# A mixture of experts behind a Hyena and Fourier mixer: the two last experts from different groups, multiplied in undivided float32, with the final norm's reads and writes moved

## The chip, the cores and the metric

The kernel runs on one core of a Trainium2 chip. The metric is the device time of one execution in microseconds, as a median of several runs, smaller being better. A profiled execution gives the trace that the rows below come from; its span is counted from its first instruction. The engines are TensorE (PE in the rows, PEld for its weight loads), VectorE (DVE), ScalarE (ACT), GpSimd (POOL) and SyncE (SP). SP and GpSimd also issue transfers, and each takes its instructions in its own order.

## What is computed

One block on 2048 rows of 1024 float32 numbers: a mixer (long convolution by FFT on half of the channels, a Fourier transform on the other half) added to the input, then a mixture of experts, then a norm over each row.

```python
g_sel = jnp.argmax(g_logits, axis=-1)              # one of 4 groups per row
top_l, top_i = lax.top_k(e_logits, TOP_K)          # 2 of its 8 experts
weight = p_group[:, None] * jax.nn.softmax(top_l, axis=-1)
...
    a = xb @ w_gate[e]                             # 1024 x 512
    u = xb @ w_up[e]
    y = (jax.nn.silu(a) * u) @ w_down[e]           # 512 x 1024
...
x = x + hierarchical_moe(rmsnorm(x, norm2_g[i]), w_group[i], ...)
return rmsnorm(x, final_g)
```

A row belongs to one group, and both of its experts are of that group. So two experts of different groups have no row in common.

## The kernel before, in words

The mixer takes the first 960 us or so and leaves the normed rows in DRAM (XR) and the sum to which the experts' results are added (X2). Then the 32 experts follow one another. Their order is found on the chip (`order`, line 1164): experts are ranked by their number of rows, and slots 0 to 31 of the kernel take them in an order that mixes those with many rows (ranks 2 to 17) with the others (`_ranks`, line 60). Below, "expert 28" means slot 28. Slots 0 and 1 are experts 0 and 1; slots 30 and 31 have the two smallest ranks' places. A slot covers 128 rows; one of the first 18 ranks has an overflow tile of 32 more (`over`, `turn_o`, `turn_so`, the second half of `extra`), whose result is added by a scatter of its own (line 1607). Rows beyond that are left to a loop at the end (line 1726), which runs as often as blocks are left over, here not at all.

For a slot e the work is this. `gather` fetches its rows from XR; `turn` (line 1531) transposes them on TensorE and splits them into a rounded part xh (a copy on ScalarE) and a rest xl (a subtraction on VectorE), both float32r, the format that TensorE multiplies in one pass. `gate_up` (line 1556) takes 8 weight tiles of 128 x 1024, each holding two slices of the contraction, and multiplies each slice three times: xh h, xh l, xl h. `cut` (line 1393) makes h and l of a weight tile: h by a copy on ScalarE (line 1397), l by a subtraction on VectorE or, for some tiles and for every second one of the last 24, on GpSimd (line 1398). The gate goes through Silu and is multiplied by the up part (lines 1573, 1574); `turn_s` transposes and splits the result; `down` (line 1642) takes 4 tiles, again with three products each. The result is scaled by the rows' weights (line 1660) and added to X2 by a scatter that accumulates (line 1661, issued by GpSimd).

`take` hands out weight tiles in the order of `seq`, which is that of `turns`: (e, 0) is gate and up of e, (e, 1) its down. Up to slot 29 the down part of e - 1 stands behind gate and up of e, with the transposes of later slots in its middle (`between`). At each call `take` also starts loads up to 28 tiles ahead and cuts 2 tiles ahead, and calls the next closure of `ends`, if there is one. A float32 tile lies in one of 16 buffers "wr" or 8 others, and the loads are issued on SP.

The end. Slots 30 and 31 don't add to X2 by an accumulating scatter. `ahead` gathers their rows of X2 (za), `finish` (line 1481) adds the weighted result to it, writes za back to X2, and norms it to oa. For the other rows `bulk` (line 1435) makes 30 steps: all 2048 rows are read from X2 in 16 blocks (`read`, into buffers "wr", line 1443), squared with their sum on ScalarE (line 1433), and in groups of four the roots are made (`rsq`, line 236) and the rows scaled on VectorE (line 1459) and written to the output by SP (line 1460). Steps start behind expert 29's down part, one at each `take`, and those left over follow at the end. Last, two scatters put oa of slots 30 and 31 over their rows of the output (line 1717); each waits for all that was written there before.

Instructions reach an engine mostly in the order in which the code makes them; the framework that allocates buffers and sets the semaphores may put a ready one ahead of one that its plan sees waiting. The line `tc.add_manual_dep(... "cuts first")` holds a square back behind cuts.

Of the kernel before, what the change touches and what calls it, by code (L numbers as in the profile page):

```python
# [46 lines left out]
FIRST = 14  # L47
NLAST = 2
# [4 lines left out]
TAIL_CUTS = tuple(range(360, 384, 2))  # L53
# [6 lines left out]
def _ranks():  # L60

    n, few = NE - NFIX - NLAST, NE - NOV - NLAST
# [142 lines left out]
def build(tc, I, out, dbg=None, upto=99):  # L205
# [4 lines left out]
    with es:  # L210
# [641 lines left out]
        turns += [(z - 1, 1), (z, 0), (z, 1), (z + 1, 0), (z + 1, 1)]  # L852
# [53 lines left out]
        with ExitStack() as e3:  # L906
# [202 lines left out]
            with tc.tile_pool(name="pd", bufs=1, side="right", reuse_waits="tile") as pd_:  # L1109
# [54 lines left out]
                def order():  # L1164
# [8 lines left out]
                    V.scalar_tensor_tensor(so[:, 0], cnt, float(NE), srt[:, 0:NE], op0=ALU.mult, op1=ALU.add)  # L1173
                    V.tensor_tensor(so[:, 1], so[:, 0], srt[:, 2 * NE:3 * NE], op=ALU.mult)
# [214 lines left out]
        if True:  # L1389
# [3 lines left out]
            def cut(n):  # L1393
# [4 lines left out]
                x = (G if n in POOL_CUTS + TAIL_CUTS else V).tensor_tensor(l, raws[n], h, op=ALU.subtract)  # L1398
# [4 lines left out]
            done, cuts = [NRAW, 0, 0], []  # L1403

            def take():
# [14 lines left out]
                return hl.pop(n), raws.pop(n)  # L1420
# [14 lines left out]
            def bulk():  # L1435
# [3 lines left out]
                scales = []  # L1439
# [5 lines left out]
                def sq(o):  # L1445
# [3 lines left out]
                    x = square(xts[o], fss[g][0][:, o - g:o - g + 1])  # L1449

                    tc.add_manual_dep(x.ins, cuts[-1].ins.name, ORDER_ONLY, reason="cuts first")
                    if o == g + n - 1:
                        rsq(fss[g][1], fss[g][0], 1.0 / D, mp, n, "q%d" % n)
                        scales.extend(range(g, g + n))

                def scale(o):
# [24 lines left out]
            def finish(e, py, za):  # L1481

                ss = mp.tile([P, 1], F32, name="zs")
                ra = mp.tile([P, 1], F32, name="zra")
# [136 lines left out]
            def turn_s(e):  # L1621
# [5 lines left out]
                for j in range(4):  # L1627
                    T.transpose(pt[:, j, :], s[:, P * j:P * j + P], ident)  # L1628
# [209 lines left out]
```

## Time and profile before

| | us |
|---|---|
| median of 3 runs (1729.77 to 1732.64) | 1729.94 |
| profiled execution, timed | 1725.99 |
| its span | 1724.2 |
| TensorE busy | 1601.3 (93%) |
| VectorE busy | 1224.2 (71%) |
| ScalarE busy | 1039.7 (60%) |
| GpSimd busy | 476.6 (28%) |
| granted clock, mean share of 2.4 GHz | 0.961 |

Busy times are those of instructions; two that overlap on an engine count once. The span ends when the last engine has passed the closing barrier. A row of the timeline has the start, the duration of what was merged into it, engine, line, operation, result <- operands, the count, and in brackets the idle time before it with what ended that. X stands for X2 in the rows, out_y for the output.

### The profile page before, as it was taken

The numbers are of one execution on the slowest core, as the hardware profiler recorded it, in microseconds if no ns is written. First come the engines' busy times: TensorE is split into PE (matmuls) and PEld (weight loads), VectorE is DVE, ScalarE is ACT, GpSimd is POOL, SyncE is SP. The second block draws the span as 40 slices with busy tenths as digits, with TensorE's granted clock in tenths as the row PEclk, the third lists the DMA queues.
The fourth block names the chain that finished last, engine by engine and source line by source line (L and its number), as shares of the span: only waits on it lengthen the run. The fifth ranks groups of instructions, "written<-read, shape, count | busy, mean of one in ns | idle before, by whom it ended". The sixth has DMA issues, their size and how long they took to land.

```text
span 1724.2 us, 27277 instructions
## 1 busy us (share of the span) xinstructions
PE 1601.3 (93%) x9043; PEld 1233.2 (72%) x9043; DVE 1224.2 (71%) x2105; ACT 1039.7 (60%) x1694; POOL 476.6 (28%) x513
## 2 busy tenths in 40 slices
PE   7999999999998979999999899999999999999853
PEld 5766766788887858877777677777777777777632
DVE  7566555423699775455889978888888888888566
ACT  8444555455698743214444567777777777777653
POOL 0202544232233232004443332221222122222252
PEclk9999999999999979999999799999999999999976
DMA  7245676798665595568678599999999999999975
GB/s 257 82 124 151 194 228 191 212 308 240 206 207 176 166 305 203 180 199 244 208 248 281 178 323 349 338 354 335 344 353 348 356 344 355 331 339 349 372 266 202
DMA packets 201853, 450.31 MB, mean 261 GB/s; under 512 B 27020, under 2 KB 82277, under 8 KB 200557
## 3 DMA queue, kind: packets, MB, share of 16 engines
q1 hardware_dynamic: 131476, 324.64, 53.0%
q0 software_dynamic: 36384, 97.94, 20.3%
q10 hardware_dynamic: 33848, 25.95, 4.7%
q8 instruction: 73, 1.20, 0.3%
q14 instruction: 72, 0.58, 0.1%
HBM read 346.32 MB, written 103.43 MB: 261 GB/s over the span
## 4 chain that ended last, share of the span: by engine, by line
PE 65%; DVE 10%; DMA 5%; issue 4%; ACT 3%; POOL 2%; ACTq 0%; SPq 0%; POOLq 0%; DVEq 0%
PE pa L1569 19%; PE py L1653 9%; PE psd L959 8%; PE psm L321 6%; PE po L1585 4%; PE pm L657 2%; PE po L1603 2%; PE psEO L1354 2%; PE pstr L1539 2%; PE psk L486 1%; PE psEO L981 1%; DVE xt L1459 1%; PE psm L657 1%; POOL acc L494 1%; PE pstr L1628 1%
## 5 line engine op out<-in xcount | busy, mean ns | idle before, releaser
L1398 DVE TENSOR_TENSOR l<-w,h 128x1024 fp32r<-128x1024 f32 x370 | 455.6, 1242 | 100.3 <-ACT h L1397 84.7
L1397 ACT CAST h<-w 128x1024 fp32r<-128x1024 f32 x384 | 402.0, 1048 | 140.0 <-PE pa L1569 86.5
L321 PE MATMUL psm<-hhi,wt 128*128 128x512 f32 x768 | 250.7, 397 | 0.7 <-ACT hhi L423 0.5
L1569 PE MATMUL pa<-l,xh 128*128 128x512 f32 x512 | 207.6, 405 | 26.2 <-POOL l L1398 14.6
L1569 PE MATMUL pa<-h,xh 128*128 128x512 f32 x512 | 208.0, 407 | 2.8 <-ACT h L1397 2.8
L1569 PE MATMUL pa<-h,xl 128*128 128x512 f32 x512 | 205.4, 401 | 0.0
L321 PEld LDWEIGHTS psm<-hhi,wt 128*128 128x128 f32 x768 | 144.3, 189 | 43.4 <-issue 11.5
L321 PE MATMUL psm<-hlo,wt 128*128 128x512 f32 x384 | 151.8, 395 | 0.4 <-DVE hlo L424 0.4
L1569 PEld LDWEIGHTS pa<-l,xh 128*128 128x128 f32 x512 | 98.9, 193 | 51.0 <-POOL l L1398 16.6
L890 POOL DMA_INDIRECT xg<-XR,gia x30 | 45.8, 1527 | 299.4 <-PE pstr L1539 194.2
L1569 PEld LDWEIGHTS pa<-h,xh 128*128 128x128 f32 x512 | 98.8, 193 | 36.4 <-ACT h L1397 8.1
L1569 PEld LDWEIGHTS pa<-h,xl 128*128 128x128 f32 x512 | 99.0, 193 | 22.4 <-DVE xl L1541 0.2
L1653 PE MATMUL py<-h,sh 128*128 128x512 f32 x256 | 105.1, 410 | 3.9 <-ACT sh L1629 3.9
L1653 PE MATMUL py<-h,sl 128*128 128x512 f32 x256 | 103.9, 408 | 3.9 <-DVE sl L1630 3.9
L1653 PE MATMUL py<-l,sh 128*128 128x512 f32 x256 | 106.2, 415 | 0.0
L321 PEld LDWEIGHTS psm<-hlo,wt 128*128 128x128 f32 x384 | 72.5, 189 | 20.4 <-issue 5.3
L1607 POOL DMA_INDIRECT X<-yo,sib x18 | 35.6, 1978 | 158.1 <-DVE l L1398 112.1
L718 POOL TENSOR_TENSOR yl<-yl,yh 128x512 fp32r<-128x512 f32 x32 | 48.9, 1532 | 105.0 <-ACT yh L717 86.7
L345 ACT COPY u<-psm 128x512 f32<-128x512 f32 x48 | 28.0, 584 | 81.1 <-PE psm L321 76.9
L494 POOL TENSOR_TENSOR acc<-ab,acc 128x512 f32<-128x512 f32 x32 | 48.3, 1509 | 68.1 <-ACT ab L493 66.8
L1585 PE MATMUL po<-w,xot 128*32 128x256 f32 x1152 | 65.7, 380 | 0.0
L1653 PEld LDWEIGHTS py<-h,sh 128*128 128x128 f32 x256 | 49.1, 192 | 15.3 <-ACT sh L1629 4.5
(465 smaller groups left out, 3673.4 us busy)
## 6 DMA issues: line engine op xcount, KB each, us to landing
w<-in_w_gate SPq DMA_DIRECT2D x128, 512.0 KB
w<-in_w_up SPq DMA_DIRECT2D x128, 512.0 KB
w<-in_w_down SPq DMA_DIRECT2D x120, 512.0 KB
xt<-in_x SPq DMA_DIRECT2D x31, 512.0 KB
de<-in_c_decay SPq DMA_DIRECT2D x32, 256.0 KB
YK<-yk ACTq DMA_DIRECT2D x32, 256.0 KB
z<-zT POOLq DMA_DIRECT2D x32, 256.0 KB, 5.7
YZ<-yz SPq DMA_DIRECT2D x64, 128.0 KB
```

Of the source, the lines that this page charges most:

```text
L321: T.matmul(pm, wt[:, a, d, :], b[q][:, d, :], start=n == 0, stop=n == 23)
L494: G.tensor_tensor(KS["acc"], ab, KS["acc"], op=ALU.add)
L657: T.matmul(pm, a[q][:, d, P * o:P * o + P], b[:, d, :], start=n == 0, stop=n == 23)
L718: e.tensor_tensor(yl, y, yh, op=ALU.subtract)
L890: G.indirect_dma_start(xg_[e], None, XR, bass.IndirectOffsetOnAxis(ap=ga[:, e:e + 1], axis=0))
L959: T.matmul(pd, a[:, c, :], b[:, c, 512 * h:512 * h + 512], start=n == 0, stop=n == 11)
L1397: cuts.append(A.copy(h, raws[n]))
L1398: x = (G if n in POOL_CUTS + TAIL_CUTS else V).tensor_tensor(l, raws[n], h, op=ALU.subtract)
L1569: T.matmul(pa[m], x[:, 4 * k + c, :], y[:, f], start=d == 0 and q == 0, stop=d == 7 and q == 2)
L1585: T.matmul(po_[e][32 * j:32 * j + 32, 256 * m:256 * m + 256], xoT[e][:, b % 2, 2 * k + b // 2, :], w[:, 256 * j:256 * j + 256], start=b == ...
L1607: G.indirect_dma_start(X4, bass.IndirectOffsetOnAxis(ap=sib[:, d:d + 1], axis=0), yo, None, compute_op=ALU.add)
L1653: T.matmul(py[i], x[:, c, :], y[:, f], start=c == 0 and q == 0, stop=c == 3 and q == 2)
```

## The change

The change has these parts.

- The order of the experts: the expert with the fewest rows of each group goes to the end of the ranks (its key is lowered by 2^18), so the last four slots hold one of each group, and the last two no common rows. `_ranks` keeps slot 29 out of the mixing too, by which slot 28 has no overflow tile and slot 27 has one.
- Slots 30 and 31 are multiplied in float32 without a split: no `cut` for the last 24 tiles, no xl and sl, one product instead of three. Copies of the transposes are shared between ScalarE and VectorE.
- The turns at the end are (30 gate and up), (31 gate and up), (30 down), (31 down), with expert 30's transposes in the middle of expert 31's gate and up, and expert 31's in the middle of expert 30's down part. The down part runs over one half of the columns and then the other.
- za of both slots is gathered behind expert 29's scatter. All 16 reads of X2 are issued there too, one behind the other.
- The squares are handed out one by one from the ninth `take` on; the first group of four is normed and scaled in the 13th; the other three groups behind gate and up of 31, behind the down part of 30 and behind that of 31. The scaled blocks are written by GpSimd's queue instead of SP's.
- `finish` squares each half right behind its addition.

```diff
-    n, few = NE - NFIX - NLAST, NE - NOV - NLAST
+    n, few = NE - NFIX - NLAST - 1, NE - NOV - NLAST - 1
...
-        turns += [(z - 1, 1), (z, 0), (z, 1), (z + 1, 0), (z + 1, 1)]
+        turns += [(z - 1, 1), (z, 0), (z + 1, 0), (z, 1), (z + 1, 1)]
...
+                    low = pd_.tile([P, 4, 1], F32, name="low")
+                    key = so[:, 0].rearrange("p (g e) -> p g e", g=4)
+                    V.tensor_reduce(low, key, axis=AX.X, op=ALU.min)
+                    V.tensor_tensor(so[:, 1].rearrange("p (g e) -> p g e", g=4), key, low.to_broadcast([P, 4, 8]), op=ALU.is_equal)
+                    V.scalar_tensor_tensor(so[:, 0], so[:, 1], -float(1 << 18), so[:, 0], op0=ALU.mult, op1=ALU.add)
...
-                x = (G if n in POOL_CUTS + TAIL_CUTS else V).tensor_tensor(l, raws[n], h, op=ALU.subtract)
+                x = (G if n in POOL_CUTS else V).tensor_tensor(l, raws[n], h, op=ALU.subtract)
...
+            whole = next(n for n, t in enumerate(seq) if t[0] >= z)
...
-                while done[1] < min(len(seq), n + 1 + CUT_AHEAD):
+                while done[1] < min(whole, n + 1 + CUT_AHEAD):
...
-                    S.dma_start(out[0, P * o:P * o + P, :], x)
-
-                def step(k):
-                    for o in range(2 * k, min(2 * k + 2, NT)):
-                        read(o)
-                    if 0 <= k - 6 < NT:
-                        sq(k - 6)
-                    for o in range(2):
-                        if scales:
-                            scale(scales.pop(0))
-                return [lambda k=k: step(k) for k in range(30)]
+                    G.dma_start(out[0, P * o:P * o + P, :], x)
+
+                def end(g):
+                    rsq(fss[g][1], fss[g][0], 1.0 / D, mp, 4, "q4")
+                    for o in range(g, g + 4):
+                        scale(o)
+
+                for o in range(NT):
+                    read(o)
+
+                steps = [[] for k in range(24)]
+                for o in range(NT):
+                    steps[8 + o].append(lambda o=o: sq(o))
+                steps[12].append(lambda: end(0))
+                ends.extend(lambda x=x: [f() for f in x] for x in steps)
+                return [lambda g=g: end(g) for g in (4, 8, 12)]
...
                 for i in range(2):
-                    z = za[:, 512 * i:512 * i + 512]
-                    V.scalar_tensor_tensor(z, py[i], wsl[:, 0, e:e + 1], z, op0=ALU.mult, op1=ALU.add)
+                    f = slice(512 * i, 512 * i + 512)
+                    V.scalar_tensor_tensor(za[:, f], py[i], wsl[:, 0, e:e + 1], za[:, f], op0=ALU.mult, op1=ALU.add)
+                    A.activation(oa[:, f], za[:, f], AF.Square, accum_out=ss[:, i:i + 1])
                 G.indirect_dma_start(X2, at(sia[:, e:e + 1]), za, None)
-                A.activation(oa, za, AF.Square, accum_out=ss)
...
+                    if e >= z:
+                        (V.tensor_copy if h else A.copy)(xh.bitcast(F32)[:, 4 * h:4 * h + 4, :], pt)
+                        continue
...
+                            if e >= z:
+                                T.matmul(pa[m], xh.bitcast(F32)[:, 4 * k + c, :], w[:, f], start=d == 0, stop=d == 7)
+                                continue
...
+                if e >= z:
+                    ws = [take()[1] for c in range(4)]
+                    for i in range(2):
+                        if i:
+                            mid()
+                        for c in range(4):
+                            T.matmul(py[i], sh.bitcast(F32)[:, c, :], ws[c][:, 512 * i:512 * i + 512], start=c == 0, stop=c == 3)
+                    return py
...
                 if not d:
-                    late = gate_up(e)
-                    if e >= z:
-                        turn_s(e)
+                    late = gate_up(e, (lambda: turn_s(z)) if e > z else None)
+                    if e > z:
+                        scaled.pop(0)()
...
                 elif e == z - 1:
-                    down(e, lambda e=e: turn(e + 2))
-                    ends.extend(bulk())
-                    za = ahead(z)
+                    down(e, lambda: turn(z + 1))
+                    zas = [ahead(x) for x in (z, z + 1)]
+                    scaled = bulk()
                 else:
-                    y = down(e, lambda: None)
-                    oas.append(finish(e, y, za))
-                    if e == z:
-                        za = ahead(e + 1)
+                    y = down(e, lambda e=e: turn_s(z + 1) if e == z else None)
+                    scaled.pop(0)()
+                    oas.append(finish(e, y, zas.pop(0)))
```

## Rows read from the trace of the kernel before

**Rows 1.** Busy time by stretch: us, then each engine, granted clock, DMA share, GB/s.
```profile
1200.00:1400.00 200.00, 200.00 (x1346) 151.97 (x1348) 165.09 (x175) 148.39 (x178) 46.06 (x31) 1.00 0.97 345
...
1620.00:1640.00 20.00, 12.48 (x47) 9.45 (x46) 8.39 (x6) 9.64 (x12) 10.42 (x5) 0.83 1.03 355
...
1660.00:1680.00 20.00, 7.95 (x25) 5.05 (x23) 16.94 (x19) 16.11 (x27) 9.81 (x4) 0.66 0.56 221
1680.00:1700.00 20.00, 10.49 (x27) 7.46 (x28) 19.20 (x30) 14.65 (x24) 7.71 (x3) 0.59 0.61 234
```

**Rows 2.** Groups of instructions, 1615 to 1724: busy us, mean ns | idle before.
```profile
L1398 POOL TENSOR_TENSOR l<-w,h 128x1024 fp32r<-128x1024 f32 x12 | 33.1, 2815 | 21.1 <-ACT h L1397 17.4 <-DMA xt<-X 3.7
L1397 ACT CAST h<-w 128x1024 fp32r<-128x1024 f32 x25 | 26.1, 1042 | 23.4 <-POOL l L1398 7.7 <-DMA xt<-X 7.1 <-PE py L1653 5.1
L1398 DVE TENSOR_TENSOR l<-w,h 128x1024 fp32r<-128x1024 f32 x13 | 22.6, 1746 | 19.9 <-ACT h L1397 19.9
L1459 DVE SCALAR_TENSOR_TENSOR xt<-xt,frs,fgb 128x1024 f32<-128x1024 f32 x16 | 21.6, 1409 | 0.4
L1433 ACT ACTIVATE jk<-xt 128x1024 f32<-128x1024 f32 x16 | 16.8, 1052 | 0.1
...
L1433 ACT ACTIVATION_READ_ACCUMULATOR jk<-xt 128x1 f32 x16 | 3.0, 188 | 0.0
L1488 DVE SCALAR_TENSOR_TENSOR za<-py,wsl,za 128x512 f32<-128x512 f32 x4 | 2.8, 743 | 0.3 <-PE py L1653 0.3
...
L1492 DVE SCALAR_TENSOR_TENSOR oa<-za,zra,fgb 128x1024 f32<-128x1024 f32 x2 | 2.6, 1284 | 0.1
L245 ACT ACT_TABLE_LOAD x2 | 2.6, 1283 | 0.0
```

**Rows 3.** Timeline of GpSimd, 1615 to 1634: the scatters to X2.
```profile
1615.03 1.55 POOL L1661 DMA_INDIRECT X<-yt,sia  x1 [20.11 <-ACT yt L1660]
1625.11 1.74 POOL L1607 DMA_INDIRECT X<-yo,sib  x1 [8.53 <-DMA X<-yt,sia]
...
1633.38 1.55 POOL L1661 DMA_INDIRECT X<-yt,sia  x1 [1.83 <-ACT h L1397]
```

**Rows 4.** Chain that ended last, in order of time: start, us, what.
```profile
1595.21 11.29 PE pa L1569 x48
...
1615.03 9.34 DMA X<-yt,sia
...
1625.11 7.55 DMA X<-yo,sib
...
1705.44 3.06 DMA out_y<-xt
...
1709.32 3.23 DMA out_y<-oa,sia
```

**Rows 5.** Timeline of SP's issues, 1620 to 1706.
```profile
1625.00 4.18 SPq L881 DMA_DIRECT2D w<-in_w_down  x4
1642.10 20.68 SPq L1443 DMA_DIRECT2D xt<-X  x16
1672.06 33.71 SPq L1460 DMA_DIRECT2D out_y<-xt  x16
```

**Rows 6.** Timeline of TensorE: an undivided float32 product, and the end of expert 29.
```profile
100.94 1.07 PE L567 MATMUL psk<-zt,fw 33*64 33x512 f32 x2
...
1621.97 0.40 PE L1653 MATMUL py<-h,sl 128*128 128x512 f32 x1
```

**Rows 7.** Timeline of VectorE: an operation of the sort, then scaling groups.
```profile
966.41 2.76 DVE L1162 TENSOR_SCALAR gib<-f,cpt 128x32 int32<-128x32 f32 x1
...
1670.75 6.97 DVE L1459 SCALAR_TENSOR_TENSOR xt<-xt,frs,fgb 128x1024 f32<-128x1024 f32 x4
...
1699.05 0.16 DVE L240 TENSOR_SCALAR q4v<-fss 128x4 f32<-128x4 f32 x1
...
1700.54 4.87 DVE L1459 SCALAR_TENSOR_TENSOR xt<-xt,frs,fgb 128x1024 f32<-128x1024 f32 x4
```

More of the change, by code (lines that the diff above doesn't have):

```diff
@@ L52 @@
 POOL_CUTS = (3, 5)
-TAIL_CUTS = tuple(range(360, 384, 2))
 ORDER_ONLY = mybir.DependencyInfo(mybir.DependencyClass.NoSync, mybir.DependencyReason.DATA)
@@ L1416, in take @@
                     done[0] += 1
-                while done[1] < min(len(seq), n + 1 + CUT_AHEAD):
+                while done[1] < min(whole, n + 1 + CUT_AHEAD):
                     cut(done[1])
                     done[1] += 1
-                return hl.pop(n), raws.pop(n)
+                return hl.pop(n, None), raws.pop(n)
             def pstr():
@@ L1448, in sq @@
                         fss[g] = mp.tile([P, n], F32, tag="fss%d" % g, name="fss"), mp.tile([P, n], F32, tag="frs%d" % g, name="frs")
[L1449 to L1454, printed above, removed]
+                    square(xts[o], fss[g][0][:, o - g:o - g + 1])
                 def scale(o):
@@ L1481, in finish @@
             def finish(e, py, za):
[L1483 to L1484 removed]
+                ss = mp.tile([P, 2], F32, tag="zs", bufs=2, name="zs")
+                ra = mp.tile([P, 1], F32, tag="zra", bufs=2, name="zra")
                 oa = mp.tile([P, D], F32, tag="yt", bufs=2, name="oa")
                 for i in range(2):
[L1487 to L1488 removed]
+                    f = slice(512 * i, 512 * i + 512)
+                    V.scalar_tensor_tensor(za[:, f], py[i], wsl[:, 0, e:e + 1], za[:, f], op0=ALU.mult, op1=ALU.add)
+                    A.activation(oa[:, f], za[:, f], AF.Square, accum_out=ss[:, i:i + 1])
                 G.indirect_dma_start(X2, at(sia[:, e:e + 1]), za, None)
[L1490 to L1491 removed]
+                V.tensor_tensor(ss[:, 0:1], ss[:, 0:1], ss[:, 1:2], op=ALU.add)
+                rsq(ra, ss[:, 0:1], 1.0 / D, mp, 1, "qa")
                 V.scalar_tensor_tensor(oa, za, ra, fgb, op0=ALU.mult, op1=ALU.mult)
@@ L1563, in gate_up @@
                     for c in range(4):
-                        (h, l), w = take()
+                        cuts_, w = take()
+                        h, l = cuts_ or (None, None)
                         for k in range(2):
@@ L1628, in turn_s @@
                     T.transpose(pt[:, j, :], s[:, P * j:P * j + P], ident)
+                if e >= z:
+                    A.copy(sh.bitcast(F32), pt)
+                    return
                 A.copy(sh, pt)
@@ L1644, in down @@
                 py = [ps.tile([P, 512], F32, tag="D", bufs=4, name="py") for i in range(2)]
+                if e >= z:
+                    ws = [take()[1] for c in range(4)]
[5 more added lines that the diff above has]
+                    return py
                 many = RANK[e] < NOV
@@ L1655, in down @@
                         mid()
-                if e >= NE - NLAST:
-                    return py
                 yt = mp.tile([P, D], F32, tag="yt", bufs=2, name="yt")
@@ L1712, in build @@
                     S.dma_start(fgb, I["final_g"].partition_broadcast(P))
-            while ends:
-                ends.pop(0)()
             for e, oa in zip((z, z + 1), oas):
```

2 lines of the change are left out of this document (removed).

## The prediction

> **What bounds the kernel now.** I read the stretches first, then the groups of the last 110 us, then the chain of waits and the queues there. Up to the last experts TensorE is the bound: from 1200 to 1400 us it is busy all 200 us at full clock [rows 1], and it stays so until expert 29's down product ends near 1622 [rows 6]. Everything the change touches, but for the order of the experts, lies in the 102 us behind that. There TensorE is half idle: busy 12.5 of 20 us from 1620, 8.0 from 1660, 10.5 from 1680, with the granted clock falling to 0.59, while VectorE rises to 19.2 of 20 [rows 1].
>
> What fills that tail is seen in the groups [rows 2]: 25 rounding copies on ScalarE (26.1 us), the subtractions that make the low parts, 13 on VectorE (22.6 us, 1746 ns each) and 12 on GpSimd (33.1 us), and beside them the 16 squares (1052 and 188 ns) and 16 scalings of the final norm (1409 ns). The products of experts 30 and 31 wait for subtractions, and those stand in queues behind the norm's work, so nothing in the tail runs at its own pace.
>
> The other thing that sets the tail is when X2 is complete. GpSimd's queue sends expert 28's scatter at 1615.0, expert 28's overflow scatter at 1625.1 (it waited 8.5 us for the first), expert 29's at 1633.4 [rows 3]; the first two take 9.34 and 7.55 us to land [rows 4]. The sums are read from 1642.1 on, the last of 16 issues is 20.7 us later, and the 16 writes of the output stretch over 33.7 us from 1672.1 [rows 5]. The last write lands 3.06 us after 1705.44, at 1708.5; the first of the two closing scatters then takes 3.23 us to 1712.55 [rows 4]. From there to the span's end at 1724.2 are 11.7 us (second scatter, its landing, the program's end), which no edit touches.
>
> **The change, part by part.** The sum is made against the profiled execution: span 1724.2 us, 1725.99 us as timed. The median shown is 1729.94, 4.0 above that; I carry the difference of spans over to the median.
>
> *Cuts removed.* 24 tiles lose their rounding (24 x 1.04 = 25 us of ScalarE) and subtraction (half on VectorE, half on GpSimd). The splits of the two experts' activations go too. None of this has a substitute, so both engines are left with the norm's own work.
>
> *Products.* Three products of a split pair become one undivided float32 product. Now 48 products take 11.29 us [rows 4], 0.235 each, so 0.70 for three, though one lasts 0.40 [rows 6]: 0.165 is overlap with the next. The nearest undivided row is a 128x64 by 512 product, recorded as two passes, 1.07 us [rows 6]; less the same overlap 0.90. Bounds 0.70 (as now) and 1.07; I take 0.90, since that row streams as many columns. The two experts have 48 such products: 43 us against 34 now. Without waits TensorE would go from 1622.4 through both gate/up pairs (2 x 14.4 us, and 0.45 of transposes) to 1651.7, and through both down products to 1666.5. What hides the extra 9 us is VectorE's chain below, which needs the first down result at 1668 and the second at 1684; if that cover went, the end would move by what TensorE is late.
>
> *Expert order.* Expert 28 has no overflow rows now; the last one that has is expert 27. So the overflow scatter between 1625 and 1633 goes, while one of the same kind leaves a turn earlier, into a queue that idles 20.1 us there [rows 3]. Overflow work on TensorE is only moved; expert 28's scatter leaves some 1.9 us later, as the 32 small products that stood behind its down product now stand ahead: 1616.9. It lands at 1626.3, the next issue follows 0.7 us behind (as 1624.4 to 1625.1 now), at 1627.0, and lands 8.7 us later (as 1633.4 to 1642.1 now): the sums can be read from 1635.7, 6.4 us earlier. Bounds 1634.5 (with 7.55) and 1642.1 (no gain). Counted from the reference's inputs, the groups' smallest experts have 113, 116, 91 and 103 rows (experts 0 and 1 keep their places), and 128 fit without overflow; so the loop for left-over rows stays empty as now. Three small VectorE operations enter the sort of the experts, on the path to the first lists; by the 0.16 us of the tiny operation in [rows 7] with gaps: 0.6 us, added in full.
>
> *Reads together.* All 16 reads are issued in a row on SP, each into a buffer whose float32 weights TensorE must have used: the eighth at 1637, the 16th at 1651.7. The queue's pace when full is (4.18 - 0.33) / 3 = 1.28 us per 512 KB [rows 5]. Nothing stands behind the reads on SP, since the writes go to GpSimd's queue. There the two reads of the experts' own rows come first, then writes in fours, the two scatters to X2, the two closing scatters; the order is that in which VectorE produces them, so a waiting write holds up only what is due later.
>
> *The chain in the new tail.* First landing after 3.1 us (as a write of this size [rows 4]), three more sums and the two gathers at 1.28: 1645.2. The fourth square ends 1.24 later, a fifth stands ahead of the root (1.24), a table load costs 1.28 [rows 2]: 1649.0; the root chain takes 1.49 [rows 7]: scaling starts near 1650.4. Then VectorE is never free for long: four scalings 4.9 [rows 7], expert 31's gate times up 0.7 (a half row like those below), second group 1.5 + 4.9, third group 6.4: 1668.8. Finishing expert 30: two halves at 0.74, half a square with its sum 0.8, sum and root 1.7, scaling 1.28 [rows 2]: 5.3, to 1674.1. ScalarE makes the last four squares only behind that root (1671.9 + 5.0), so VectorE waits 2.8; last group 6.4: 1683.3; finishing expert 31: 1688.6. The last write lands 3.1 us after the last scaling, as now (1705.41 to 1708.5), at 1686.4; the first closing scatter leaves 0.8 later, as 1708.5 to 1709.3 now, and lands at 1690.4; with the 11.7 us that nothing touches 1702.1, and 0.6 for the sort: **1702.7**. Against 1724.2 that is 21.5 us less, so 1729.9 - 21.5 = **1708.4 us**.
>
> *Bounds that are left.* A scaling took 1.22 in [rows 7]'s clean group and 6.97 / 4 = 1.74 beside GpSimd's subtractions; I take 1.22, since those are gone, the other end being + 8 us. A write issued by GpSimd could land like a scatter (7.55), + 4.5 us. The 2.8 us of waiting for the last squares, and the 1.5 of two root chains, vanish if other work is placed into them: - 5.8. Squares could be placed behind the experts' work on ScalarE: + 5.
>
> **Rivals.** *TensorE becomes the bound.* The clock was granted at 0.59 to 0.66 while TensorE stood half idle [rows 1]. If the float32 stretch ran at the lower level (1.2 GHz), a product would cost 1.8 and the 48 of them 86.4 us: TensorE done at 1709.3, expert 31 finished 5.3 later, and with the second closing scatter to the end 11.7: 1726.3, with the sort 1726.9, so 1732.6 us, no change. Against it: the stretch has no wait ahead of its products, and every dense stretch stands at 1.00 [rows 1].
>
> *VectorE and GpSimd block each other, and the kernel becomes slower.* Place: the 16 scalings, beside the 16 writes that GpSimd now has to issue instead of SP. For it: a 128x32 operation took 2.76 us, where tiny ones take 0.16, and a scaling group 6.97 where another took 4.87 [rows 7]; in both cases GpSimd worked beside it. Price: with 16 scalings at 3.0 us, 16 x 1.78 = 28.5 us more, 1736.9 us. It decides from (1733.4 - 1708.4) / 16 = 1.56 us more per scaling, 2.8 us each. Against it: GpSimd's work there was subtractions of 2.8 us [rows 2], and issuing is shorter and 16 times only.
> The Trainium skill (SBUF — State Buffer, section Who interferes with whom) says that a VectorE instruction with two SBUF inputs contends with a GpSimd instruction that reads SBUF, and not with one that only writes there, and that a DMA held up by VectorE is one whose descriptors GpSimd makes. By that rule the scalings keep 1.22 us and it is the writes that could be held up; the slow group beside subtractions agrees, and no row shows a scaling beside a plain write from GpSimd.
>
> *The sums come no earlier, or the squares wait.* If expert 29's scatter lands at 1642 as now, or ScalarE's order holds the squares back, VectorE's chain starts 6 to 11 us later: 1714 to 1719 us, still faster. For it: the scatters compete with weights, whose DMA share is full until 1640 [rows 1].
>
> **How the numbers follow.** Chain as summed: 0.78. Sums or squares late: 0.12. TensorE at the lower level: 0.04. Blocking: 0.05. The rest, 0.01, is that the sort changes nothing in the tail. The forecast is the first case's 1708.4. Its bounds reach from - 5.8 and - 1.2 (1701.4) to + 8, or to + 4.5 with 5 (1718); the range takes in the late sums with one of these on top, and a little below for orders of the work that I have not thought of: 1698 to 1721. What a measurement of this kernel tells from no change is about 0.2%, 3.5 us. Faster: the first two cases, 0.90. Same: TensorE at the lower level and the rest, 0.05. Slower: blocking, 0.05.
>
> **What would show it.** Right: no rounding or subtraction behind 1622, TensorE dense at full clock from 1622 to 1650 at about 0.90 per product, reads from about 1636, first scaling near 1650, scalings in fours of 4.9 us with VectorE nearly full until 1689, last write landing near 1686, the same 15 us behind it. Wrong: float32 products far from 0.90, reads starting at 1642, scalings above 1.7 us, writes that land late behind GpSimd, or VectorE waiting for squares in the first three groups.

## The result and the profile after

The changed kernel takes 1708.11 us (median of 4 runs, 1706.25 to 1710.97) against 1730.08 (4 runs, 1729.77 to 1732.64): a ratio of 0.9872, 95% interval 0.9859 to 0.9886, or 22 us less. Its profiled execution has a span of 1704.4 us (timed 1706.25), where the prediction had 1702.7 (and 1708.4 for the median). The size came out right, in part by luck: four terms of the sum were off, by + 3.8 us (the reads start late), - 5.5 (VectorE's chain is shorter), + 2.9 (the last write lands late) and - 1.7 (the program's end is shorter), and they cancel to - 0.5. What bounds the new tail is not what I took it to be.

But for the order of the experts and its sort, all that differs by design lies behind expert 30's first product (1622.2 us before, 1625.2 after; it is 672.4 us behind the experts' first product in both). In the texts below "t" counts from that product: the span ends at t 102.0 before and t 79.3 after, 22.7 us less.

The stretches, as in [rows 1]:

```profile
1200.00:1400.00 200.00, 200.00 (x1335) 152.64 (x1334) 165.23 (x175) 148.16 (x177) 46.65 (x29) 1.00 0.96 343
1620.00:1640.00 20.00, 20.00 (x63) 10.93 (x62) 2.61 (x3) 3.10 (x5) 3.87 (x2) 1.00 1.04 373
1640.00:1660.00 20.00, 18.38 (x46) 7.99 (x44) 4.08 (x9) 11.06 (x19) 2.85 (x4) 1.00 1.02 393
1660.00:1680.00 20.00, 10.94 (x24) 4.70 (x24) 19.45 (x43) 13.29 (x32) 6.75 (x12) 0.85 1.03 408
1680.00:1700.00 20.00, 0.00 (x0) 0.00 (x0) 6.25 (x9) 0.00 (x0) 5.96 (x7) 0.50 0.63 254
```

TensorE is dense at full clock to 1658 instead of half idle from 1622. VectorE is full only from 1657 to 1686. The last but one column is new in the reading: the DMA share is above 1.0 up to 1680, where before had 0.56 from 1660 and 0.61 from 1680 [rows 1].

Within the stretch from 1660 TensorE waits, and its clock falls for a while; from its timeline, and from finer stretches:

```profile
1653.07 5.31 PE L1670 MATMUL py<-w,sh 128*128 128x512 f32 x12
1662.46 0.66 PE L1644 MATMUL pstr<-ident,s 128*128 128x128 f32 x4 [4.07 <-DVE s L1590]
1662.95 10.45 PE L1670 MATMUL py<-w,sh 128*128 128x512 f32 x20
```

```profile
1664.00:1666.00 2.00, 2.00 (x4) 0.82 (x3) 1.96 (x3) 1.97 (x6) 0.37 (x1) 0.50 1.02 418
1666.00:1668.00 2.00, 2.00 (x4) 0.72 (x3) 2.00 (x3) 1.97 (x3) 0.70 (x2) 0.69 1.03 420
1668.00:1670.00 2.00, 2.00 (x6) 0.95 (x5) 1.74 (x4) 1.22 (x4) 1.06 (x2) 1.00 1.02 420
```

The groups behind 1615, as in [rows 2]:

```profile
L1582 PE MATMUL pa<-w,xh 128*128 128x512 f32 x64 | 27.8, 592 | 0.0
L1462 DVE SCALAR_TENSOR_TENSOR xt<-xt,frs,fgb 128x1024 f32<-128x1024 f32 x16 | 19.5, 1281 | 0.1
L1442 ACT ACTIVATE jk<-xt 128x1024 f32<-128x1024 f32 x16 | 16.9, 1054 | 17.6 <-DMA xt<-X 17.4
L1670 PE MATMUL py<-w,sh 128*128 128x512 f32 x32 | 15.8, 651 | 0.0
L1405 DVE TENSOR_TENSOR l<-w,h 128x1024 fp32r<-128x1024 f32 x4 | 4.9, 1222 | 1.3 <-ACT h L1404 1.2
L1404 ACT CAST h<-w 128x1024 fp32r<-128x1024 f32 x3 | 3.1, 1045 | 0.6 <-PE py L1680 0.6
```

Of 25 rounding copies 3 are left (of expert 29), of 13 and 12 subtractions 4. A product is recorded as two instructions: 32 gate and up products in 27.8 us, 0.87 each.

GpSimd's scatters, as in [rows 3], then SP's issues, as in [rows 5]:

```profile
1600.54 1.57 POOL L1686 DMA_INDIRECT X<-yt,sia  x1 [0.30 <-issue]
1612.27 2.03 POOL L1623 DMA_INDIRECT X<-yo,sib  x1 [10.16 <-DMA X<-yt,sia]
1620.90 2.32 POOL L1686 DMA_INDIRECT X<-yt,sia  x1 [6.60 <-ACT h L1404]
1633.03 1.55 POOL L1686 DMA_INDIRECT X<-yt,sia  x1 [9.81 <-ACT s L1589]
```

```profile
1621.67 11.68 SPq L882 DMA_DIRECT2D w<-in_w_down  x8
1642.34 16.30 SPq L1451 DMA_DIRECT2D xt<-X  x16
```

The overflow scatter of 27 leaves only at 1612.3, as it waits for 27's own to land. Expert 28's follows at 1620.9 and 29's at 1633.0, and the reads begin at 1642.3, t 17.2, no earlier by the clock than before.

VectorE's scalings, as in [rows 7], and the end of the chain, as in [rows 4]:

```profile
1656.93 4.87 DVE L1462 SCALAR_TENSOR_TENSOR xt<-xt,frs,fgb 128x1024 f32<-128x1024 f32 x4
1664.05 4.87 DVE L1462 SCALAR_TENSOR_TENSOR xt<-xt,frs,fgb 128x1024 f32<-128x1024 f32 x4
1671.46 4.87 DVE L1462 SCALAR_TENSOR_TENSOR xt<-xt,frs,fgb 128x1024 f32<-128x1024 f32 x4
1679.43 4.87 DVE L1462 SCALAR_TENSOR_TENSOR xt<-xt,frs,fgb 128x1024 f32<-128x1024 f32 x4
```

```profile
1684.60 5.67 DMA out_y<-xt
1690.42 0.53 issue
1690.98 0.20 issue
1691.18 3.26 DMA out_y<-oa,sia
```

First scaling at t 31.8, last one done at t 59.1, last write landed at t 65.1. The DMA view of 1620 to 1700 (40 slices of 2 us, the digit the busy tenths of the 16 engines) shows best what changed. Before:

```profile
DMA  9999999999149999999999800057390639920899
```

After:

```profile
DMA  9999999999999999999999999999999999915040
```

Before, the transfers stood still for about a quarter of these 80 us, and nearly half of the time behind 1664. After, they run without a gap until the last write lands at 1690.

### The profile page after: what moved, and what is told of

It reads as the page before. It is cut to its first block, busy times and chain, and to the rows that moved or that the text cites. A ratio compares the mean times of both kernels' runs of the same rounds, so it can differ in the third digit from the quotient of the medians.

```text
span 1704.4 us, 27090 instructions
## 1 busy us (share of the span) xinstructions
PE 1596.5 (94%) x8995; PEld 1217.7 (71%) x8995; DVE 1194.8 (70%) x2094; ACT 1014.3 (60%) x1670; POOL 456.5 (27%) x517
## 4 chain that ended last, share of the span: by engine, by line
PE 67%; DVE 9%; DMA 6%; issue 3%; ACT 3%; POOL 2%; ACTq 0%; SPq 0%; POOLq 0%; DVEq 0%
PE pa L1585 20%; PE py L1680 10%; PE psd L960 8%; PE psm L322 6%; PE po L1601 4%; PE pm L658 2%; PE po L1619 2%; PE pstr L1548 2%; PE psEO L1361 2%; PE psk L487 1%; PE psEO L982 1%; PE pa L1582 1%; POOL acc L495 1%; PE pstr L1644 1%; PE psk L510 1%
## 5 line engine op out<-in xcount | busy, mean ns | idle before, releaser
L1405 DVE TENSOR_TENSOR l<-w,h 128x1024 fp32r<-128x1024 f32 x358 | 436.4, 1231 | 82.0 <-ACT h L1404 59.1
L1404 ACT CAST h<-w 128x1024 fp32r<-128x1024 f32 x360 | 377.1, 1049 | 117.4 <-PE pa L1585 85.3
L1585 PE MATMUL pa<-l,xh 128*128 128x512 f32 x480 | 189.6, 395 | 3.6 <-DVE l L1405 3.6
L1585 PE MATMUL pa<-h,xh 128*128 128x512 f32 x480 | 192.8, 402 | 0.0
L1585 PE MATMUL pa<-h,xl 128*128 128x512 f32 x480 | 189.2, 394 | 0.0
L1585 PEld LDWEIGHTS pa<-h,xh 128*128 128x128 f32 x480 | 90.7, 189 | 30.3 <-issue 11.1
L1585 PEld LDWEIGHTS pa<-l,xh 128*128 128x128 f32 x480 | 91.1, 190 | 24.0 <-DVE l L1405 4.5
L1585 PEld LDWEIGHTS pa<-h,xl 128*128 128x128 f32 x480 | 91.1, 190 | 20.8 <-DVE xl L1553 0.2
L1680 PE MATMUL py<-h,sl 128*128 128x512 f32 x240 | 96.0, 401 | 0.0
L346 ACT COPY u<-psm 128x512 f32<-128x512 f32 x48 | 28.1, 585 | 81.2 <-PE psm L322 81.2
L658 PE MATMUL pm<-wh,hhi 128*128 128x256 f32 x208 | 58.8, 283 | 0.0
```

Source lines behind the costliest of these rows:

```text
L658: T.matmul(pm, a[q][:, d, P * o:P * o + P], b[:, d, :], start=n == 0, stop=n == 23)
L1404: cuts.append(A.copy(h, raws[n]))
L1405: x = (G if n in POOL_CUTS else V).tensor_tensor(l, raws[n], h, op=ALU.subtract)
L1585: T.matmul(pa[m], x[:, 4 * k + c, :], y[:, f], start=d == 0 and q == 0, stop=d == 7 and q == 2)
L1680: T.matmul(py[i], x[:, c, :], y[:, f], start=c == 0 and q == 0, stop=c == 3 and q == 2)
```

## The experiments

Executions differ in the part ahead of the experts: their first product stands at 949.8 us in the profile of before, at 952.8 after, and from 951.5 to 960.8 in the other twelve, though no edit touches that part. Medians of few runs carry some of this. So the tail is read in t, beside the ratio to the kernel before. `back_last` below came out with the same order as the changed kernel and ended at t 79.0 instead of 79.3: the one repeat that there is of t. Each t is read from one profiled execution.

| | reads from | first scaling | last group from | last write landed | end, t | ratio to before (95%) |
|---|---|---|---|---|---|---|
| before | 19.9 | 48.5 | 78.3 | 86.3 | 102.0 | |
| changed | 17.2 | 31.8 | 54.3 | 65.1 | 79.3 | 0.9872 (0.9859 to 0.9886) |
| split_kept | 16.8 | 45.7 | 74.1 | 83.8 | 98.0 | 0.9943 (0.9922 to 0.9963) |
| undivided_alone | 19.9 | 34.8 | 56.1 | 67.9 | 84.1 | 0.9888 (0.9869 to 0.9908) |
| old_ranks | 19.6 | 34.5 | 57.9 | 68.9 | 83.1 | 0.9883 (0.9865 to 0.9902) |
| ranks_two | 13.8 | 33.7 | 56.6 | 66.9 | 81.1 | 0.9887 (0.9869 to 0.9904) |
| writes_on_sp | 17.2 | 31.8 | 54.3 | 66.4 | 82.2 | 0.9858 (0.9834 to 0.9882) |
| half_writes | 17.1 | 31.7 | 55.2 | 62.6 | 76.8 | 0.9849 (0.9817 to 0.9881) |
| half_scalings | 17.0 | 31.7 | 52.7 | 65.1 | 79.2 | 0.9864 (0.9836 to 0.9893) |
| half_both | 17.1 | 31.7 | 51.8 | 57.6 | 71.8 | 0.9827 (0.9806 to 0.9848) |
| za_late | 17.1 | 29.5 | 55.5 | 65.9 | 80.0 | 0.9877 (0.9848 to 0.9906) |
| no_back | 17.1 | 31.7 | 54.2 | 64.2 | 78.7 | 0.9876 (0.9857 to 0.9894) |
| back_last | 17.0 | 31.9 | 54.4 | 64.8 | 79.0 | 0.9864 (0.9832 to 0.9896) |
| pool_scales | 17.1 | 31.7 | 58.3 | 67.9 | 82.1 | 0.9892 (0.9863 to 0.9921) |

**Which part of the change brings the time.** `split_kept` is the changed kernel with the split:

```diff
-            whole = next(n for n, t in enumerate(seq) if t[0] >= z)
+            whole = len(seq)
...
-                            if e >= z:
-                                T.matmul(pa[m], xh.bitcast(F32)[:, 4 * k + c, :], w[:, f], start=d == 0, stop=d == 7)
-                                continue
```

> The changed kernel with experts 30 and 31 still in three products of split pairs: their 24 cuts come back (rounding on ScalarE, subtractions half on VectorE, half on GpSimd), the down part runs over contraction slices again; the order of the experts, the turns, the reads, squares and writes stay changed. Theory: most of the 22 us came from what the cuts took from the engines that also make the norm, 25 us of ScalarE and some 21 us of VectorE in the tail (rows 2), so most comes back: 1718 to 1728 us, and VectorE's scalings start later than the 31.8 us after expert 30's first product that the changed kernel shows. Rival: the gain came from the order of the tail (squares and groups interleaved, turns swapped) and the split had only filled idle engines: 1708 to 1713 us.

```profile
1673.73 6.97 DVE L1462 SCALAR_TENSOR_TENSOR xt<-xt,frs,fgb 128x1024 f32<-128x1024 f32 x4
1674.34 2.89 POOL L1405 TENSOR_TENSOR l<-w,h 128x1024 fp32r<-128x1024 f32 x1 [5.22 <-ACT h L1404]
```

Above, from the timelines of VectorE and GpSimd in this run: the first scalings, 13.9 us later in t, four in 6.97 us beside a subtraction on GpSimd. Median 1724.6 us, end at t 98.0: the split costs 18.7 us there, as the theory had it. The times make it less: 0.9943 against the changed kernel's 0.9872 is 12 us. The profile is of the longest of this kernel's four executions (1727.73 us, the others 1722.85 to 1725.95); why t and the times differ by so much here stays open. The other way round, `undivided_alone` is the kernel before with the undivided products alone:

```diff
-                while done[1] < min(len(seq), n + 1 + CUT_AHEAD):
+                while done[1] < min(whole, n + 1 + CUT_AHEAD):
...
+                            if e >= z:
+                                T.matmul(pa[m], xh.bitcast(F32)[:, 4 * k + c, :], w[:, f], start=d == 0, stop=d == 7)
+                                continue
```

> The kernel before with one part of the change alone: experts 30 and 31 in undivided float32 (their cuts and low parts gone, one product for three, the down part by halves of the columns). Order of the experts, turns, za, reads, squares, scalings and SP's writes stay as before. Theory: this is the main part of the change, as putting the split back took 18.7 us in the tail of the trace; with the old order of turns (gate and up of 31 behind down of 30, the second za behind the write-back) a little is left: 1709 to 1714 us, 16 to 21 less than before. Rival: the interleaving is what makes room for the norm, and the undivided products alone give 10 us or less: 1720 or more.

Median 1713.1 us, end at t 84.1, 17.9 us less than before (19 by the ratio). The other parts alone (`split_kept`) bring 102.0 - 98.0 = 4.0 in t, and 10 by the ratio. In t the two add up to 21.9 of the 22.7 us, as if the parts hardly needed each other; by the ratios they add up to 29 of 22, as if they overlapped. That the undivided products are the main part holds by both; whether the parts add up is not settled. No run separates the other parts (turns, early gathers, pace of the squares) from each other, but for the ranks below. In the old order of turns TensorE waits 11.4 us for expert 31's gate:

```profile
1676.78 1.12 PE L1636 MATMUL pstr<-ident,s 128*128 128x128 f32 x4 [11.44 <-DVE s L1582]
```

**The order of the experts.** Two kernels with another number of slots kept out of the mixing, `old_ranks` and `ranks_two`:

```diff
-    n, few = NE - NFIX - NLAST - 1, NE - NOV - NLAST - 1
+    n, few = NE - NFIX - NLAST, NE - NOV - NLAST
```

```diff
-    n, few = NE - NFIX - NLAST - 1, NE - NOV - NLAST - 1
+    n, few = NE - NFIX - NLAST - 2, NE - NOV - NLAST - 2
```

> The changed kernel with the old mixing of ranks: slot 28 has an overflow tile again, slot 27 none; all else as changed, the last two experts still of different groups. In the changed kernel expert 28's scatter stood waiting from about 1619 to 1620.9 for the overflow scatter of 27 and took 12.1 us to land, expert 29's left at 1633.0 and the reads began at 1642.3, where I had reckoned 1635.7 (and 3 us more, by which the mixer's part of that run was late). Theory now: the moved overflow scatter was not free, it only changed places in a chain of four scatters; putting it back costs 2 to 4 us: 1710 to 1712 us, the reads 19 to 21 us after expert 30's first product instead of 17.2. Rival, the step of the prediction: 6.4 us, 1714.5 us. Second rival: nothing, 1707 to 1709.

The reads begin 2.4 us later, the end comes 3.8 us later in t, of which 1.2 may be given back ahead of expert 30 (671.2 us from the experts' first product instead of 672.4; kernels with the changed order have 671.5 to 672.4). In the trace that is the theory's 2 to 4, not the prediction's 6.4. The times cannot tell them apart: the median is 1713.5 us, past the theory's 1712 and under the rival's 1714.5, and the intervals of the two ratios overlap.

> The changed kernel with slots 28 and 29 both kept out of the mixing of ranks, so that the last slot with an overflow tile is 26 instead of 27. Theory: the chain of accumulating scatters sets the start of the reads, each waiting for the landing of the one before; with 27's overflow scatter out of the way expert 28's leaves when it is ready, some 2 us earlier, expert 29's when its own result is ready or at 28's landing, and the reads begin 1 to 4 us earlier than 17.2 us after expert 30's first product; transfers and VectorE's chain both start from there, so the end comes earlier by as much: 75.5 to 78.3 instead of 79.3, 1704 to 1707 us. Rival 1: the scatters land later by what they leave earlier, since they share the transfers with the weights: no change. Rival 2: overflow work is now denser in the earlier slots and TensorE loses there what the tail gains: the tail is shorter, the time is not.

The reads begin 3.4 us earlier, and the end is 1.8 us later in t. From SP, ScalarE and VectorE of this run:

```profile
1625.77 11.82 SPq L882 DMA_DIRECT2D w<-in_w_down  x8
1642.31 20.63 SPq L1451 DMA_DIRECT2D xt<-X  x16
...
1653.63 1.06 ACT L1442 ACTIVATE jk<-xt 128x1024 f32<-128x1024 f32 x1 [17.44 <-DMA xt<-X]
...
1662.18 4.87 DVE L1462 SCALAR_TENSOR_TENSOR xt<-xt,frs,fgb 128x1024 f32<-128x1024 f32 x4
```

The reads are issued 4.7 us behind the last weights instead of 9.0, and the first block is there 11.3 us after its issue instead of 4.4; the next squares then follow without a wait. So the earlier issue brought no earlier block: rival 1, and worse than it. Expert 28's scatter left 1.0 us earlier in t, and 29's 3.2. That it is the weights that the first block waited for was not tested by a run, but the packets of the trace fit it: the last 8 MiB of the queue that loads, which are the 16 blocks if it works in the order of its issues, start at t 20.6 here, 6.8 us behind the first issue, and at t 19.0 in the changed kernel, 1.8 behind it.

**What bounds the new tail.** `half_writes`, `half_scalings` and `half_both` take half of the bytes written, of VectorE's scalings, and of both. They leave out part of the output and serve to time the tail alone:

```diff
-                    G.dma_start(out[0, P * o:P * o + P, :], x)
+                    G.dma_start(out[0, P * o:P * o + P, 0:512], x[:, 0:512])
```

```diff
-                    V.scalar_tensor_tensor(x, x, fss[g][1][:, o - g:o - g + 1], fgb, op0=ALU.mult, op1=ALU.mult)
+                    V.scalar_tensor_tensor(x[:, 0:512], x[:, 0:512], fss[g][1][:, o - g:o - g + 1], fgb[:, 0:512], op0=ALU.mult, op1=ALU.mult)
```

> The changed kernel, writing only the first 512 of 1024 columns of the 16 scaled blocks (the other columns of the output are left out); reads, squares and scalings whole. Theory: the new tail is bound by transfers; 4.2 MB less at 408 GB/s is 10 us of transfer, so the last read lands some 4 us earlier, the last two squares no longer wait, the last group is scaled 3 to 5 us earlier and its write lands in about 3 us: 5 to 8 us, 1700 to 1703 us. Rival, VectorE's chain is the bound as in the prediction: the groups are scaled at the same times after expert 30's first product (31.8, 38.9, 46.3, 54.3 us) and only the last landing is shorter: 1705.5 us.

```profile
1692.06 2.29 DMA out_y<-xt
```

The groups stand where they were, or 0.9 us later, the last write lands in 2.29 us instead of 5.67, and the end gains 2.4 us, not the theory's 5 to 8. That looked like VectorE's chain, and the next run was to show it:

> The changed kernel, scaling only the first 512 of 1024 columns of the 16 blocks on VectorE (the other columns are written unscaled); reads, squares and writes whole. All times from expert 30's first product; in the changed kernel the first scaling stands at 31.8, the last group at 54.3 to 59.1, the last write lands at 65.1, the span ends at 79.3 us. Theory, VectorE's chain is the bound (as the run with half the writes left the groups where they were): 16 x 0.6 us less work; the last squares, at 50.2, then hold the last group, which starts near 52 and takes 2.5: last scaling 4 to 5 us earlier, end at 74.5 to 76. Rival, the transfers: the last landing stays past 64 and the end at 78 or more, with each write landing later after its issue.

From the end of its chain and of VectorE's timeline:

```profile
1682.01 9.30 DMA out_y<-xt
```

```profile
1678.97 2.74 DVE L1462 SCALAR_TENSOR_TENSOR xt<-xt,frs,fgb 128x512 f32<-128x512 f32 x4
```

VectorE is done 3.7 us earlier, and the last write lands at t 65.1 all the same, in 9.30 us instead of 5.67: the rival, transfers, to the tenth of a microsecond. So my theory of that moment fell. What fits both runs is two bounds side by side, the transfers first and VectorE's chain some 2 us behind:

> The changed kernel scaling and writing only the first 512 columns of the 16 blocks (the other columns of the output are left out). Half the scalings alone left the end at 79.2 us after expert 30's first product (79.3 in the changed kernel), half the writes alone brought it to 76.8 with VectorE's groups where they were. Theory: transfers and VectorE's chain are two bounds side by side, so the two together give much more than 0 + 2.4: the last blocks are read some 2 us earlier, the last group is scaled near 50 in 2.7 us and lands in 2.3, expert 31 is finished near 54, and the closing part of 14 us follows: end at 67 to 71. Rival: a third thing stands close behind (expert 31's down product, which ends at 48 to 49, with its finish, or the reads themselves), and the end stays at 73 or more.

```profile
DMA  9999999999999999999999999893688231300000
```

End at t 71.8, 7.5 us less where the two alone give 2.4 and 0 (just outside the expected 67 to 71). In the DMA view of 1620 to 1700 the transfers now fall off from 1670 on. What ends last there is the reads: the square of the 16th block waits for it until 1672.1, t 48.6, only 0.4 us earlier than in the changed kernel, where the theory had some 2.

Three smaller runs move or remove single transfers. `za_late` holds the gathers of the two experts' own rows back (its edit and that of `pool_scales` below are written out here over more lines than in the kernel):

```diff
                 za = mw.tile([P, D], F32, tag="xg", bufs=2, name="za")
+                G.tensor_copy(za[:, 0:1], xts[3][:, 0:1])
...
-                    zas = [ahead(x) for x in (z, z + 1)]
                     scaled = bulk()
+                    zas = [ahead(x) for x in (z, z + 1)]
```

> The changed kernel with the two gathers of the experts' own rows of X2 held until the fourth block has been read (GpSimd copies one element of that block into each of the two tiles ahead of its gather); the rest of the order is the same on every engine. Theory: the first four blocks landed about 2 us apart (squares at 1646.8, 1648.6, 1651.2, 1653.2) because 1 MB of gathers ran beside them, where 1.28 was the pace in rows 5; without them the first scaling comes 1.5 to 2.5 us earlier than 31.8 after expert 30's first product, and as VectorE's chain is full from there, so does the end: 77 to 78 instead of 79.3. Rival: the first blocks are slow for another reason (the landing of the last weights or of a read itself): first scaling within 0.5 us of 31.8, or the sums of expert 30 now wait for the gathers, past 45.4, and the end is no earlier.

The first scaling does come 2.3 us earlier, but the end 0.8 later, so the theory's end failed. What fits is that the gathers' bytes are moved from ahead of the first blocks to ahead of the last, whose squares come at t 47.9 and 50.4 instead of 46.5 and 49.0. `back_last` was to move the write-backs of those rows behind the output's writes:

```diff
-                G.indirect_dma_start(X2, at(sia[:, e:e + 1]), za, None)
...
+            for e, za in backs:
+                G.indirect_dma_start(X2, at(sia[:, e:e + 1]), za, None)
```

> The changed kernel with the two write-backs of the experts' rows into X2 behind all writes of the output on GpSimd's queue, ahead of the closing scatters. In the changed kernel the first one waited 5.1 us for the last reads of X2, and the third group's four writes stood behind it until 1676.0, 3.3 us after the first of them was scaled. Theory: VectorE's chain is the bound, so this frees only transfers: last landing 0 to 1.5 us earlier, end at 78 to 79.5 us after expert 30's first product. Rival 1: the queue was a bound, the last write lands 3 us earlier: 76. Rival 2: the write-backs now lie ahead of the closing scatters and cost 1 to 3 us there: 80 to 82.

It tells nothing of its question: the first write-back left ahead of the third group's writes, as before the edit. `no_back` leaves both out:

```diff
-                G.indirect_dma_start(X2, at(sia[:, e:e + 1]), za, None)
```

> The changed kernel without the two write-backs of the experts' 30 and 31 rows into X2, which only the loop for left-over rows would read, and that runs no time here. Two runs stand against each other: half the scalings left the last landing at 65.1 us after expert 30's first product and the end at 79.2, half the writes took 2.4 us off. Theory from both: the transfers set the last landing, and VectorE's chain stands 2.4 us behind them as the next bound. The write-backs are some 0.9 MB, 2.3 us at 385 GB/s, and the third group's writes stood 3.3 us behind the first: end 1.5 to 2.5 us earlier, 76.8 to 77.8 after expert 30's first product. Rival: they fill gaps of the transfers and cost nothing: 79 to 79.5.

The third group's writes now follow their scalings at once, and the last write lands 0.9 us earlier, with the end at t 78.7: between theory and rival, as the groups on VectorE stay where they are.

**Which queue writes, and blocking.** `writes_on_sp` changes one letter:

```diff
-                    G.dma_start(out[0, P * o:P * o + P, :], x)
+                    S.dma_start(out[0, P * o:P * o + P, :], x)
```

> The changed kernel with the 16 writes of the output issued by SP instead of GpSimd. Theory: the tail is bound by what the transfers carry (DMA share 1.02 and 1.03 from 1640 to 1680), so the queue hardly matters; group 3's writes no longer stand behind GpSimd's write-back of expert 30's rows (issued at 1674.87, 2 us after the group's first scaling was done), which gives 0 to 2 us: 1706 to 1708 us, the last write still landing over 4.5 us after its issue. Rival: writes issued by GpSimd land late (5.67 us where SP's last one took 3.06 in rows 4), so SP gives 2.6 us: 1705.5, landing in about 3 us. Second rival, blocking between VectorE and GpSimd: scalings get faster than 1.22 us.

```profile
1683.56 7.26 DMA out_y<-xt
...
1691.64 3.24 DMA out_y<-oa,sia
1694.88 0.02 issue
```

The median is 1708.6 us. The scalings stay at 1.22 us, the last write takes 7.26 us to land instead of 5.67, and from the landing of the first closing scatter to the end of the span it is 11.7 us, as in both kernels in which SP writes (before and `undivided_alone`), where all kernels with GpSimd's writes have 10.0 to 10.2. So neither rival, nor the theory's gain of up to 2 us. The profile has SP 2.9 us behind; the times (0.9858) do not show it, and I leave that open. The Trainium skill (DMA: Bandwidth & Descriptors, section Rules for kernel authors) says that spreading transfers over the issuing engines brings no bandwidth, since all use the same 16 DMA engines; the last landings here, t 66.4 from SP and t 65.1 from GpSimd, agree in that SP's queue brought none.

`pool_scales` puts a GpSimd computation beside the scalings:

```diff
-                    V.scalar_tensor_tensor(x, x, fss[g][1][:, o - g:o - g + 1], fgb, op0=ALU.mult, op1=ALU.mult)
+                    if o in (3, 7, 11):
+                        A.mul(x, x, fss[g][1][:, 3:4])
+                        G.tensor_tensor(x, x, fgb, op=ALU.mult)
+                    else:
+                        V.scalar_tensor_tensor(x, x, fss[g][1][:, o - g:o - g + 1], fgb, op0=ALU.mult, op1=ALU.mult)
```

> The changed kernel with the last block of each of the first three groups scaled elsewhere: by the root on ScalarE, by the gain on GpSimd (one product of 128x1024 there, beside VectorE's scalings). A test of the rival that VectorE and GpSimd block each other. Theory: they do where GpSimd computes, not where it only issues: a scaling beside such a product takes about 1.7 us instead of 1.22 (6.97 us for four in rows 7, beside subtractions), so of the 3 x 1.2 us taken from VectorE only 1 to 2 come through: end at 77.5 to 79.5 us after expert 30's first product. Rival 1: no blocking, scalings stay at 1.22, 3.7 us less: 75.6. Rival 2: ScalarE's extra passes hold up squares or GpSimd's products hold up writes: 80 or more.

VectorE's first two groups and GpSimd's products:

```profile
1657.75 5.86 DVE L1462 SCALAR_TENSOR_TENSOR xt<-xt,frs,fgb 128x1024 f32<-128x1024 f32 x3
...
1666.24 3.68 DVE L1462 SCALAR_TENSOR_TENSOR xt<-xt,frs,fgb 128x1024 f32<-128x1024 f32 x3
...
1658.98 2.35 POOL L1462 TENSOR_TENSOR xt<-xt,fgb 128x1024 f32<-128x1024 f32 x1 [12.92 <-ACT xt L1462]
...
1670.76 2.36 POOL L1462 TENSOR_TENSOR xt<-xt,fgb 128x1024 f32<-128x1024 f32 x1
```

Three scalings take 5.86 us with the product beside them and 3.68 without: 2.18 us more, nearly the product's whole 2.35. The writes of the first group's scaled blocks stood behind the product as well. End at t 82.1, the second rival's side, and the blocking of the theory. By the rule of the Trainium skill that the prediction cited (SBUF — State Buffer, section Who interferes with whom) a scaling, which has two SBUF inputs, contends with a GpSimd instruction that reads SBUF; this trace agrees. GpSimd's issues of writes did not slow the scalings of the changed kernel, which follow one another at 1.22 us.

No version that does all the work beat the changed kernel by more than the measurement can tell: `no_back` ends 0.6 us earlier in t, but leaves out what the loop for left-over rows would need. "Reads together" was not run as a change of its own, so what it brings is not shown. The closing scatters wait for each other (issued 4.1 us apart), though their rows cannot overlap; no run takes that wait away.

## Why the prediction was right, and where its steps were off

- *Cuts removed*: right, and, together with the one product for three, the main part: 17.9 to 18.7 of 22.7 us in t, 12 to 19 of 22 by the ratios.
- *Products*: 0.90 us taken, 0.87 measured at full clock; gate and up of both experts done at t 28.1 (forecast 29.3, with its transposes). The Trainium skill (FP8 and Floating Point Precision, section TensorE Precision Notes) gives true float32 four passes; by that and the 0.235 us of a product in [rows 4], taken as one pass, an estimate is 0.94, and the trace, with 0.87, is near it. TensorE then stood 4.1 us waiting for expert 31's gate, whose product on VectorE was behind the first scalings. Behind that wait its last ten products took 1.05 us each, where the six ahead of it took 0.89, and it ended at t 48.2 instead of 44.1, still hidden.
- *Expert order* is the step that failed: "the sums can be read from 1635.7, 6.4 us earlier" (t 13.3, counted from the 1622.4 of the forecast). They began at t 17.2, 2.7 us earlier in t than before, and by the clock at 1642.3, which the prediction itself had named as a sign of being wrong. I let the overflow scatter of 27 leave "into a queue that idles", and did not ask when 27's own scatter lands: it left at 1600.5 and held the overflow one to 1612.3, and expert 28's to 1620.9; 29's left 12.1 us behind that, where 28's had taken 9.34 to land [rows 4]. In `ranks_two`, where the reads do begin near the forecast (t 13.8), the end was 1.8 us later, so the 6.4 brought nothing there.
- *The chain in the new tail*: first scaling at t 31.8 against 28.0, by the late reads alone: from their first issue it is 14.6 us, forecast 14.7. From there to the last scaling 27.4 us against 32.9: the wait of 2.8 for the last squares did not come, and expert 30's finish ran among the groups instead of between them. I had named both as bounds (- 5.8 in all).
- *Last landing and end*: 6.0 us behind the last scaling (1684.30 to 1690.27) against 3.1. The bound that I gave, "a write issued by GpSimd could land like a scatter", was the wrong reason: from SP it took 7.26, with half the bytes 2.29, and with half the scalings, issued 3.7 us earlier in t, 9.30. What fits all of these is a backlog of the transfers. The "11.7 us that nothing touches" became 10.0: with SP's writing, that one letter, it is 11.7 again. What takes the time in there is not shown.
- *What bounds the tail*: "What hides the extra 9 us is VectorE's chain" is half of it. The transfers are a second cover that stands as high: half the scalings changed the end by 0.1 us. My sum followed the one chain alone. It met the time since that chain stands only some 2 us from the other and since its own errors cancel.
- *Sort*: no trace of 0.6 us; the experts' first product to expert 30's takes 672.4 us in both.
- *Rivals*: TensorE did fall to the lower level (1.2 GHz) for a part of its last products, but not in the dense stretch that the rival was about: the granted clock is 1.00 to 1662, 0.50 from 1664 to 1666, behind the wait of 4.1 us, and 1.00 again from 1668. That cost some 1.6 us (ten products at 1.05 instead of 0.89) and was hidden. Blocking exists (`pool_scales`), but not in this change, where GpSimd only issues and the scalings kept 1.22 us. "The sums come no earlier" was half true, and its 5 us were paid back by the shorter chain: two errors of opposite sign, not a better forecast.

## What to carry to other kernels

When work is taken from engines that share a tail, ask what the transfers do next: here the gain ended where the 16 DMA engines ran without a gap, and a kernel with half of one engine's work removed took the same time. A bound is shown by halving each candidate alone and then both, since two that stand side by side hide each other. And a transfer that may leave earlier can be worth nothing while earlier ones are still on their way, as in `ranks_two`.

## What was not expected of the hardware

- The end of the program, from the landing of the first closing scatter, takes 10.0 to 10.2 us where GpSimd wrote the output and 11.7 where SP did, in all fourteen profiles.
- The accumulating scatters wait for each other: from the issue of 27's at 1600.5 to the first read at 1642.3 four of them take 41.8 us, as long as two experts' products (gate and up of 28 and 29 start 20.4 us apart, at 1580.2 and 1600.6).
- The part ahead of the experts varies by 11 us between executions (first product at 949.8 to 960.8), with no edit there.
